# A decoder layer's down projection, from plain matrix products to one level of Strassen in a hand-ordered item list

## The chip, the cores and the metric

One core of a Trainium2 chip runs the whole kernel. The metric is device microseconds of one execution; the time before is the median of three runs. A core has five engines that run side by side and meet at semaphores: TensorE (PE; its weight loads are PEld), VectorE (DVE), ScalarE (ACT), GpSimd (POOL) and SyncE (SP), which here only issues DMAs. TensorE writes its sums to PSUM, 8 banks of 128 x 512 float32; everything else works from SBUF.

## The reference, cut to what matters

One layer: a token mixer (not touched), then a gated feed-forward part on 512 tokens of width 2048, inner width 5632 (44 blocks of 128).

```python
for l in range(DEPTH):                       # DEPTH = 1
    ...
    x = x + rms_norm(m, attn_post_norm[l])
    u = rms_norm(x, ffn_pre_norm[l])
    f = (jax.nn.silu(u @ w_gate[l]) * (u @ w_up[l])) @ w_down[l]
    x = x + rms_norm(f, ffn_post_norm[l])
```

The down projection is the product with w_down, 512 x 5632 by 5632 x 2048. The final norm needs the sum of squares over all 2048 columns of a token before it can scale.

## The kernel before

All inputs are float32, and a product is made of three matmuls: each operand is split into a high part (ScalarE's rounding copy, `wh` for weights) and a remainder (VectorE's subtraction of that copy from the source, `wl`), and high x high, high x remainder and remainder x high are summed in PSUM (`mm3`, lines 120 to 122). `whi` (L100) and `wlo` (L107) do this for a weight tile of 128 x 1024, `split` (L128, L129) for an activation tile of 128 x 512.

*Gate and up* (`bridge`) already use one level of Strassen in Winograd's form: blocks of the two operands are added and subtracted, and seven half-size products take the place of eight. Their order is written by hand: `items` is a list of products, each with a weight source and a function that issues its matmuls, and tables `pre_`, `tops` and `post` hang other work on item numbers. The loop at lines 1159 to 1183 walks the list: at step i it makes the high part of item i + 2, runs `pre_[i]`, runs `tops` up to item i + 3 (weight differences on VectorE), makes the remainder of item i + 2, and then issues item i's matmuls. TensorE, VectorE, ScalarE and GpSimd keep this order; SP's order of DMAs is set by the scheduler. The activated products go out to `hd` in HBM, one 128 x 512 tile for each of the 44 blocks of the inner width (inner width by tokens).

*The down projection* (`down`) follows in ordinary scheduled code. For each of two column halves p of 1024 it walks the 44 blocks k: a weight tile is loaded and split, `hd`'s tile is loaded once and split in each half, and 4 token tiles (tt) x 2 column tiles (c) x 3 matmuls of 128 x 512 add to eight PSUM banks (lines 1230 to 1235). The last six blocks of the second half (`NLAST`) run token tile by token tile, so that the banks of one token tile are done while others still run. `evac` takes a bank's squares (ScalarE, L1215) and its product with the gain (VectorE, L1216); then a token tile's reciprocal root mean square is worked out by small VectorE operations (`rstd`), and four `scalar_tensor_tensor` (L1256) scale and add the residual before the stores (L1258).

Of the kernel before, what the change touches and what calls it, by code (L numbers as in the profile page):

```python
# [25 lines left out]
NEXT = 22  # L26
NR = 3
NHU = 30
# [3 lines left out]
NLAST = 6  # L32
# [30 lines left out]
class Net:  # L63
# [141 lines left out]
    def run(self, ctx):  # L205
# [20 lines left out]
        with tc.tile_pool(name="ext", bufs=NEXT, reuse_waits="tile") as self.M:  # L226
            self.down()
# [625 lines left out]
    def bridge(self, q01, ea):  # L853
# [293 lines left out]
        for u in (*range(NPRE, NUNIT), *range(NPRE)):  # L1147
# [8 lines left out]
            at(pre_, i + 2, hout, u)  # L1156
        srcs, his, los = [], [], []
# [27 lines left out]
    def down(self):  # L1185
        nc, t = self.nc, self.t
        hs = []

        def load(k):
            h = self.u() if k < NHU else self.mx()  # L1190
            nc.sync.dma_start(h, t["hd"][k])
            hs.append(h)

        for k in range(4):
            load(k)
        gr, x2 = [], {}
# [12 lines left out]
        def evac(p, tt, ps):
            if p == 0:  # L1210
                ssc[tt] = self.C.tile([P, 4], F32, name=f"ssc{tt}")
            for c in range(2):
                cc = p * 2 + c
                f = self.u()
                nc.scalar.activation(f, ps[c], AF.Square, accum_out=ssc[tt][:, cc:cc + 1])  # L1215
                nc.vector.tensor_tensor(f, ps[c], gr[cc], op=ALU.mult)  # L1216
                fg[tt, cc] = f

        for p in range(2):
            ps = {tt: (self.acc(), self.aux()) for tt in range(NTT)}  # L1220
            nlast = NLAST if p else 0
            for k in range(FT - nlast):
                wh, wl = self.wsplit(t["wd"][p, k])
                if p == 0 and k + 4 < FT:
                    load(k + 4)
                with self.hp():
                    hh, hl = self.split(hs[k], alloc=self.mx if p or k > 16 else self.u)
                if p == 0 and k == 24:
                    loads()
                for tt in range(NTT):  # L1230
                    ts = slice(tt * P, (tt + 1) * P)
                    for c in range(2):
                        cs = slice(c * 512, (c + 1) * 512)
                        self.mm3(ps[tt][c], hh[:, ts], hl[:, ts], wh[:, cs], wl[:, cs],
                                 k == 0, k == FT - 1)
            if not p:
                for tt in range(NTT):
                    evac(p, tt, ps[tt])
                continue
            last = []  # L1240
            for k in range(FT - nlast, FT):
                with self.hp():
                    st = self.wload(t["wd"][p, k])
                    last.append((self.split(hs[k], alloc=self.mx), [self.split(st[:, :512]),
                                                     self.split(st[:, 512:])]))
# [102 lines left out]
```

## Time and profile before

| | |
|---|---|
| median of 3 runs (lowest, highest) | 2247.0 us (2246.62, 2247.09) |
| span of the profiled execution | 2249.2 us |
| TensorE busy (matmuls), share of the span | 2213.9 us, 98% |
| VectorE busy | 1457.8 us, 65% |
| ScalarE busy | 911.3 us, 41% |
| GpSimd busy | 254.0 us, 11% |
| DMA | 299.86 MB, mean 133 GB/s |
| chain that ended last | PE 90%, DVE 5% |

The profile gives no time of its own for the profiled execution other than its span, which is 2.2 us above the median. Busy time of TensorE counts a matmul from its start to its modelled end, and matmuls overlap, so the spacing of starts tells the price of one, not the duration beside it. The same holds to a lesser degree for VectorE, whose operations start a little before the one ahead has ended.

### The profile page before, as it was taken

The numbers are of one execution on the slowest core, as the hardware profiler recorded it, in microseconds if no ns is written. First come the engines' busy times: TensorE is split into PE (matmuls) and PEld (weight loads), VectorE is DVE, ScalarE is ACT, GpSimd is POOL, SyncE is SP. The second block draws the span as 40 slices with busy tenths as digits, with TensorE's granted clock in tenths as the row PEclk, the third lists the DMA queues.
The fourth block names the chain that finished last, engine by engine and source line by source line (L and its number), as shares of the span: only waits on it lengthen the run. The fifth ranks groups of instructions, "written<-read, shape, count | busy, mean of one in ns | idle before, by whom it ended". The sixth has DMA issues, their size and how long they took to land.

```text
span 2249.2 us, 35218 instructions
## 1 busy us (share of the span) xinstructions
PE 2213.9 (98%) x14150; PEld 2005.5 (89%) x14150; DVE 1457.8 (65%) x2238; ACT 911.3 (41%) x1274; POOL 254.0 (11%) x218
## 2 busy tenths in 40 slices
PE   9999999999999999999999999999999999999998
PEld 7878887888879999999999999999999888888886
DVE  6347777535554577897888778999999623343345
ACT  5324343336553444654444444444343422232231
POOL 2012311000001665530000000000000000000000
PEclk9999899999999999999999999999999999999999
DMA  6222112232103576884333343666655744433332
GB/s 206 93 85 66 57 57 62 94 95 83 66 29 103 183 221 196 251 259 129 118 118 114 119 125 122 186 203 207 188 181 171 253 141 123 130 94 95 102 103 104
DMA packets 108340, 299.86 MB, mean 133 GB/s; under 512 B 12160, under 2 KB 29328, under 8 KB 108176
## 3 DMA queue, kind: packets, MB, share of 16 engines
q1 hardware_dynamic: 105152, 292.10, 41.6%
q10 hardware_dynamic: 3024, 5.51, 0.7%
q8 instruction: 111, 1.82, 0.3%
q14 instruction: 53, 0.43, 0.1%
HBM read 271.34 MB, written 26.21 MB: 132 GB/s over the span
## 4 chain that ended last, share of the span: by engine, by line
PE 90%; DVE 5%; POOL 1%; ACT 1%; issue 1%; DMA 1%; SPq 0%; DVEq 0%; ACTq 0%; POOLq 0%
PE acc L120 18%; PE acc L122 18%; PE acc L121 18%; PE aux L122 10%; PE aux L120 10%; PE aux L121 10%; DVE wl L107 1%; PE aux L541 1%; PE aux L755 1%; DVE u L526 1%; ACT wh L100 0%; DVE u L955 0%; PE aux L588 0%; PE aux L723 0%; PE aux L741 0%
## 5 line engine op out<-in xcount | busy, mean ns | idle before, releaser
L120 PE MATMUL acc<-u,wh 128*128 128x256 f32 (+2 forms) x2064 | 635.0, 309 | 2.6 <-ACT wh L270 1.4
L121 PE MATMUL acc<-u,wh 128*128 128x256 f32 (+2 forms) x2064 | 635.7, 308 | 0.0
L122 PE MATMUL acc<-u,wl 128*128 128x256 f32 (+2 forms) x2064 | 634.6, 308 | 0.1
L107 DVE TENSOR_TENSOR wl<-ws,wh 128x1024 fp32r<-128x1024 f32 (+2 forms) x315 | 375.5, 1193 | 305.2 <-ACT wh L100 299.0
L100 ACT ACTIVATE wh<-ws 128x1024 fp32r<-128x1024 f32 (+1 forms) x315 | 329.9, 1049 | 498.9 <-PE acc L121 141.2
L120 PEld LDWEIGHTS acc<-u,wh 128*128 128x128 f32 (+1 forms) x2064 | 395.5, 192 | 21.4 <-ACT wh L270 1.9
L122 PEld LDWEIGHTS acc<-u,wl 128*128 128x128 f32 (+1 forms) x2064 | 395.4, 192 | 19.1 <-DVE wl L107 1.0
L121 PEld LDWEIGHTS acc<-u,wh 128*128 128x128 f32 (+1 forms) x2064 | 395.8, 192 | 17.9 <-DVE u L250 0.4
L122 PE MATMUL aux<-u,wl 128*128 128x256 f32 (+1 forms) x1264 | 362.3, 287 | 1.9 <-DVE wl L107 1.9
L120 PE MATMUL aux<-u,wh 128*128 128x256 f32 (+1 forms) x1264 | 362.8, 287 | 0.3 <-ACT wh L100 0.3
L121 PE MATMUL aux<-u,wh 128*128 128x256 f32 (+1 forms) x1264 | 362.1, 286 | 0.0
L100 ACT ACTIVATE wh<-wt 128x1024 fp32r<-128x1024 f32 x176 | 186.9, 1062 | 299.1 <-PE aux L121 112.8
L122 PEld LDWEIGHTS aux<-u,wl 128*128 128x128 f32 x1264 | 243.5, 193 | 3.8 <-DVE wl L107 2.5
L120 PEld LDWEIGHTS aux<-u,wh 128*128 128x128 f32 x1264 | 243.6, 193 | 1.8 <-ACT wh L100 0.5
L121 PEld LDWEIGHTS aux<-u,wh 128*128 128x128 f32 x1264 | 243.6, 193 | 1.2
L107 DVE TENSOR_TENSOR wl<-wt,wh 128x1024 fp32r<-128x1024 f32 x176 | 215.0, 1222 | 34.0 <-ACT wh L100 33.9
L120 PE MATMUL acc<-wh,u 128*128 128x512 f32 x356 | 140.2, 395 | 0.0
L121 PE MATMUL acc<-wl,u 128*128 128x512 f32 x356 | 140.1, 394 | 0.0
L122 PE MATMUL acc<-wh,u 128*128 128x512 f32 x356 | 139.5, 394 | 0.0
L120 PE MATMUL acc<-wh,m 128*128 128x512 f32 x260 | 101.1, 389 | 0.0
L121 PE MATMUL acc<-wl,m 128*128 128x512 f32 x260 | 101.1, 389 | 0.0
L122 PE MATMUL acc<-wh,m 128*128 128x512 f32 x260 | 101.1, 389 | 0.0
(293 smaller groups left out, 3037.2 us busy)
## 6 DMA issues: line engine op xcount, KB each, us to landing
ws<-wgu_in SPq DMA_DIRECT2D x136, 512.0 KB, 3.8
wsx<-wgu_in SPq DMA_DIRECT2D x88, 512.0 KB, 3.7
ws<-wd_in SPq DMA_DIRECT2D x88, 512.0 KB, 3.7
ws<-wo_in SPq DMA_DIRECT2D x56, 512.0 KB, 3.7
ws<-wf_in SPq DMA_DIRECT2D x39, 512.0 KB, 3.6
ws<-wt_in SPq DMA_DIRECT2D x32, 512.0 KB, 3.6
hd<-g SPq DMA_DIRECT2D x44, 256.0 KB, 2.8
u<-hd SPq DMA_DIRECT2D x30, 256.0 KB, 3.9
```

The lines of the kernel that those rows point to most:

```text
L100: self.nc.scalar.activation(h, st, AF.Copy)
L107: nc.vector.tensor_tensor(lo[:, :d], st[:, :d], h[:, :d], op=ALU.subtract)
L120: mm(ps, lhsT=ah, rhs=bh, start=start, stop=False)
L121: mm(ps, lhsT=ah, rhs=bl, start=False, stop=False)
L122: mm(ps, lhsT=al, rhs=bh, start=False, stop=stop)
L526: nc.vector.tensor_tensor(qt[hs].rearrange("p (c h n s) -> p c h n s", c=NTT, h=2, s=s)[:, :, h], c3(v3(q)[:, :, 1, :]), c3(dv[:, :, 1, :] ...
L541: mm(ps[:m, c * 64:(c + 1) * 64], lhsT=kt[:, c * P:c * P + m], rhs=qt[:, c * 64:(c + 1) * 64], start=True, stop=True)
L755: mm(po[:, ts], lhsT=v[kt][:, (h % 4) * P:(h % 4 + 1) * P], rhs=pT[:, kt * P:(kt + 1) * P], start=kt == 0, stop=kt == tt)
```

## The change

The down projection becomes part of the item list. `down` and its pool are gone; `down_items` appends to `items` after the last unit of gate and up. Four blocks of the inner width make a "duo": its first and third block are one half of the inner width, its second and fourth the other, so that activations (tokens in halves of 256) and weights (columns in halves of 512, in each column half p of 1024) are 2 x 2 blocks. Eleven duos are taken two at a time in six chunks (the last has one), and for each chunk and each p come seven products in the order 1, 5, 6, 3, 7, 4, 2, each for all its duos. A product of one duo is one item: 12 matmuls of 128 x 512 into two banks. Two pairs of banks, X and Z, hold running sums, and a third pair per p collects product 2 over all chunks. At the end of a product its sum is taken from PSUM and added to one of 16 accumulators in SBUF (`evac`): by ScalarE's copy to a buffer of `gv` (four of them) and GpSimd's addition, for product 7 by VectorE straight from PSUM. The activation sums S1 to S4 (`ssum...`) and one weight difference in four (product 7) are GpSimd's; three are VectorE's. `conv` splits the activations once per duo, not once per p. At the end `stat` takes the squares and multiplies by the gain (GpSimd, for the last block VectorE), and `final` scales and stores a token tile.

```diff
-        with tc.tile_pool(name="ext", bufs=NEXT, reuse_waits="tile") as self.M:
-            self.down()
...
             at(pre_, i + 2, hout, u)
+        self.down_items(items, pre_, post, tops, at)
...
-    def down(self):
+    def down_items(self, items, pre_, post, tops, at):
...
+        def ssum13(d):
+            r = raw[d]
+            r["S1"] = self.u()
+            G.tensor_tensor(r["S1"], r["21"], r["22"], op=ALU.add)
+            G.tensor_tensor(r["21"], r["11"], r["21"], op=ALU.subtract)
+            r["S3"] = r.pop("21")
...
+        def tsum(c, p, d, n):
+            w = lambda q: W[c, p, d, q]
+            if n == 5:
+                o = w("11") if len(chunks[c]) > 1 else wtile("wt")
+                D.tensor_tensor(o, w("12"), w("11"), op=ALU.subtract)
...
+            elif n == 7:
+                G.tensor_tensor(w("12"), w("22"), w("12"), op=ALU.subtract)
...
+        def prod(c, p, n, d):
+            def f(wh, wl):
...
+                ps = bank["X" if n in (1, 6, 7) else p if n == 2 else "Z"]
...
+                for tt in range(2):
+                    for j in range(2):
+                        a = slice(j * 256 + tt * P, j * 256 + (tt + 1) * P)
+                        w = slice(j * 512, (j + 1) * 512)
...
+                        mm(hi, wh, first and j == 0, False)
+                        mm(hi, wl, False, False)
+                        mm(lo, wh, False, last and j == 1)
+            return f
+
+        EV = {1: ("C11",), 5: ("C22",), 6: ("C12",), 3: ("C12",), 7: ("C22", "C21"), 4: ("C21",)}
+
+        def evac(c, p, n):
+            ps = bank["X" if n in (1, 6, 7) else "Z"]
+            for name in EV[n]:
+                for tt in range(2):
+                    a = acc.get((p, name, tt))
+                    if a is None:
+                        a = acc[p, name, tt] = self.u()
+                        nc.scalar.copy(a, ps[tt])
+                    elif n != 7:
+                        g = self.gv()
+                        nc.scalar.copy(g, ps[tt])
+                        G.tensor_tensor(a, a, g, op=ALU.add)
+                    else:
+                        D.tensor_tensor(a, ps[tt], a, op=ALU.add)
...
+            if name == "C11":
+                D.tensor_tensor(f, bank[p][tt], f, op=ALU.add)
+            sq = self.gv()
+            nc.scalar.activation(sq, f, AF.Square, accum_out=ssc[tok][:, cc:cc + 1])
+            (eng or G).tensor_tensor(f, f, gr[cc], op=ALU.mult)
...
+        end = len(items)
+        at(pre_, end - 15, tail_loads)
...
+        for tok in (2, 3):
+            at(pre_, end, final, tok)
+        for tt in range(2):
+            at(pre_, end + 1, stat, 1, "C11", tt, D)
+        for tok in (0, 1):
+            at(pre_, end + 1, final, tok)
```

VectorE in the middle of the down projection, before: `wl` is a weight remainder, `m` the remainder of an activation tile.

```order
L107 TENSOR_TENSOR wl_19348<-ws_19344,wh_19346 128x1024
L107 TENSOR_TENSOR wl_19384<-ws_19380,wh_19382 128x1024
L129 TENSOR_TENSOR m_19681<-u_19494,m_19680 128x512
L107 TENSOR_TENSOR wl_19420<-ws_19416,wh_19418 128x1024
L129 TENSOR_TENSOR m_19717<-u_19570,m_19716 128x512
```

And of the change, in a chunk with two duos: L126 is `split`'s remainder, L104 the weight remainder, L1255 the difference t4, L1296 the addition of product 7's sum from PSUM (`acc`).

```order
L126 TENSOR_TENSOR u_20804<-u_20689,u_20803 128x512
L1255 TENSOR_TENSOR wt_20505<-wt_20662,wt_20505 128x1024
L104 TENSOR_TENSOR wl_20808<-wsx_20556,wh_20801 128x1024
L1255 TENSOR_TENSOR wt_20528<-wt_20681,wt_20528 128x1024
L104 TENSOR_TENSOR wl_20836<-wt_20505,wh_20822 128x1024
L126 TENSOR_TENSOR u_20853<-u_20714,u_20852 128x512
L104 TENSOR_TENSOR wl_20860<-wt_20528,wh_20850 128x1024
L1296 TENSOR_TENSOR u_18787<-acc_18680,u_18787 128x512
L1296 TENSOR_TENSOR u_18789<-acc_18681,u_18789 128x512
```

Beside the remainders, three weight differences in four and two accumulators' additions of every chunk and p now stand in VectorE's queue.

GpSimd's queue before ends in the output projection, ahead of gate and up: these are its last rows.

```order
L109 TENSOR_TENSOR wl_9449<-ws_9432,wh_9434 128x256
L109 TENSOR_TENSOR wl_9498<-ws_9477,wh_9479 128x256
L109 TENSOR_TENSOR wl_9536<-ws_9526,wh_9528 128x256
L109 TENSOR_TENSOR wl_9576<-ws_9564,wh_9566 128x256
L1344 UNCONDITIONAL_BRANCH
L1344 ISA
```

With the change 188 operations follow there; these are from one half of a chunk (L1294 an accumulator's addition, L1252 the weight difference of product 7, L1204 and L1205 the sums S1 and S3).

```order
L1294 TENSOR_TENSOR u_18729<-u_18729,g_20683 128x512
L1294 TENSOR_TENSOR u_18731<-u_18731,g_20686 128x512
L1252 TENSOR_TENSOR wsx_20530<-ws_20558,wsx_20530 128x1024
L1294 TENSOR_TENSOR u_18787<-u_18787,g_20739 128x512
L1294 TENSOR_TENSOR u_18789<-u_18789,g_20742 128x512
L1252 TENSOR_TENSOR wsx_20556<-ws_20580,wsx_20556 128x1024
L1294 TENSOR_TENSOR u_18832<-u_18832,g_20778 128x512
L1294 TENSOR_TENSOR u_18834<-u_18834,g_20781 128x512
L1204 TENSOR_TENSOR u_20784<-u_20691,u_20693 128x512
L1205 TENSOR_TENSOR u_20691<-u_20689,u_20691 128x512
```

GpSimd had nothing behind the output projection; now it has work through the whole down projection, all of it reading two tiles of SBUF.

VectorE at the end, before: the last token tile's bank products and the start of its norm (ahead of them the last scaling of the token tile before; `rstd`'s small operations and four scalings follow).

```order
L1256 SCALAR_TENSOR_TENSOR u_21829<-u_21829,sm_21838,u_19530 128x512
L1216 TENSOR_TENSOR u_21895<-acc_20274,u_19504 128x512
L1216 TENSOR_TENSOR u_21898<-aux_20275,u_19506 128x512
L1253 TENSOR_REDUCE sm_21901<-ssc_20261 128x1
L168 TENSOR_SCALAR sm_21903<-sm_21901 128x1
```

And of the change: L1326 scales the last tiles of token tile 3, L1314 adds product 2's bank to C11, L1317 is the gain.

```order
L1326 SCALAR_TENSOR_TENSOR u_18789<-u_18789,sm_22312,u_21895 128x512
L1326 SCALAR_TENSOR_TENSOR u_19109<-u_19109,sm_22312,u_21897 128x512
L1314 TENSOR_TENSOR u_19069<-aux_19316,u_19069 128x512
L1317 TENSOR_TENSOR u_19069<-u_19069,u_21877 128x512
L1314 TENSOR_TENSOR u_19071<-aux_19317,u_19071 128x512
L1317 TENSOR_TENSOR u_19071<-u_19071,u_21877 128x512
L1321 TENSOR_REDUCE sm_22341<-ssc_22116 128x1
```

Before, one token tile is left behind the last matmul; now token tiles 2 and 3 stand in VectorE's queue ahead of C11, and token tiles 0 and 1 behind it.

## Rows read from the trace of the kernel before

**Rows 1.** Busy us by stage: length, PE, PEld, DVE, ACT, POOL, clock, DMA share, GB/s
```profile
1400.00:1700.00 300.00, 300.00 (x2502) 300.00 (x2502) 275.58 (x340) 123.90 (x130) 0.00 (x0) 1.00 0.62 192
1762.00:2200.00 438.00, 438.00 (x1934) 362.75 (x1934) 157.55 (x172) 133.38 (x179) 0.00 (x0) 1.00 0.42 128
2200.00:2249.20 49.20, 39.59 (x175) 32.48 (x173) 26.28 (x84) 6.53 (x18) 0.00 (x0) 0.94 0.23 86
```

**Rows 2.** Timeline of PE: start, us, engine, line, operation, out<-in
```profile
1758.03 0.40 PE L120 MATMUL acc<-wh,u 128*128 128x512 f32 x1
...
1759.19 0.28 PE L122 MATMUL aux<-u,wl 128*128 128x256 f32 x1
...
1761.82 0.40 PE L120 MATMUL aux<-wh,u 128*128 128x512 f32 x1
...
2239.21 0.39 PE L122 MATMUL aux<-u,m 128*128 128x512 f32 x1
```

**Rows 3.** Groups by line, 1762 to 2239: count | busy us, mean ns | idle before
```profile
L107 DVE TENSOR_TENSOR wl<-ws,wh 128x1024 fp32r<-128x1024 f32 x80 | 98.0, 1226 | 105.9 <-ACT wh L100 105.8
L1216 DVE TENSOR_TENSOR u<-acc,u 128x512 f32<-128x512 f32 x7 | 4.8, 686 | 16.6 <-ACT u L1215 16.6
L100 ACT ACTIVATE wh<-ws 128x1024 fp32r<-128x1024 f32 x80 | 84.2, 1052 | 131.1 <-PE aux L122 124.1 <-DMA ws<-wd_in 4.4 <-PE aux L121 2.5
L129 DVE TENSOR_TENSOR m<-u,m 128x512 fp32r<-128x512 f32 x43 | 29.3, 691 | 105.6 <-ACT m L128 102.6 <-PE aux L121 3.0
```

**Rows 4.** Timeline of DVE where POOL does nothing
```profile
854.53 0.47 DVE L989 SCALAR_TENSOR_TENSOR u<-u,col,r 128x256 f32<-128x256 f32 x1
...
861.32 0.95 DVE L107 TENSOR_TENSOR wl<-ws,wh 128x768 fp32r<-128x768 f32 x1
...
1738.21 1.22 DVE L1024 TENSOR_TENSOR wt<-wsx,wt 128x1024 f32<-128x1024 f32 x1
1739.35 1.22 DVE L107 TENSOR_TENSOR wl<-wt,wh 128x1024 fp32r<-128x1024 f32 x1
...
1752.35 1.29 DVE L129 TENSOR_TENSOR u<-u,u 128x512 fp32r<-128x512 f32 x2
```

**Rows 5.** Timeline of POOL where DVE does nothing
```profile
745.00 1.29 POOL L884 TENSOR_TENSOR m<-m,u 128x512 f32<-128x512 f32 x1
```

**Rows 6.** Timeline of DVE, then of POOL, where they meet
```profile
735.29 1.48 DVE L107 TENSOR_TENSOR wl<-ws,wh 128x1024 fp32r<-128x1024 f32 x1 [2.80 <-ACT wh L100]
736.69 0.74 DVE L911 TENSOR_TENSOR u<-aux,u 128x256 f32<-128x256 f32 x2
...
738.01 2.34 DVE L107 TENSOR_TENSOR wl<-ws,wh 128x1024 fp32r<-128x1024 f32 x1
...
735.63 2.27 POOL L884 TENSOR_TENSOR m<-m,u 128x512 f32<-128x512 f32 x1
737.99 1.29 POOL L885 TENSOR_TENSOR u<-u,m 128x512 f32<-128x512 f32 x1
```

**Rows 7.** Timeline of DVE, then of POOL, both without a gap
```profile
898.84 1.48 DVE L107 TENSOR_TENSOR wl<-ws,wh 128x768 fp32r<-128x768 f32 x1
900.24 1.84 DVE L955 SCALAR_TENSOR_TENSOR u<-u,col,rm 128x256 f32<-128x256 f32 x2
902.00 1.49 DVE L107 TENSOR_TENSOR wl<-ws,wh 128x768 fp32r<-128x768 f32 x1
...
898.59 2.32 POOL L957 TENSOR_TENSOR u<-hq,u 128x256 f32<-128x256 f32 x2
900.87 0.93 POOL L109 TENSOR_TENSOR wl<-ws,wh 128x256 fp32r<-128x256 f32 x1
```

**Rows 8.** Timeline of the end: last token tile's reduction and scalings
```profile
2240.96 0.15 DVE L1253 TENSOR_REDUCE sm<-ssc 128x1 f32<-128x4 f32 x1
...
2243.46 2.74 DVE L1256 SCALAR_TENSOR_TENSOR u<-u,sm,u 128x512 f32<-128x512 f32 x4
```

**Rows 9.** Busy us by stage, columns as in rows 1
```profile
830.00:840.00 10.00, 6.93 (x59) 6.72 (x57) 2.63 (x8) 4.48 (x9) 3.21 (x3) 1.00 0.75 248
840.00:850.00 10.00, 8.14 (x47) 8.17 (x48) 5.26 (x17) 3.11 (x6) 4.83 (x5) 0.66 0.41 136
```

More of the change, by code (lines that the diff above doesn't have):

```diff
@@ L25 @@
 NMIX = 15
-NEXT = 22
 NR = 3
-NHU = 30
 NEA = 8
@@ L31 @@
 NUNIT = FT
-NLAST = 6
 LOGEXP = "natural_log_exp_and_others"
@@ new lines, in down_items, with sload @@
+        base = len(items)
+        duos = [NPRE + 4 * d for d in range((FT - NPRE) // 4)] + [4 * d for d in range(NPRE // 4)]
+        chunks = [duos[i:i + 2] for i in range(0, len(duos), 2)]
+        nchunk = len(chunks)
+        S, raw, W = {}, {}, {}
+        acc = {}
+        bank = {}
+        gr, x2, ssc = {}, {}, {}
+        D, G = nc.vector, nc.gpsimd
+        def sload(d):
+            r = raw[d] = {}
+            for n, e, hs in (("11", 0, 0), ("21", 0, 256), ("22", 1, 256), ("12", 1, 0)):
+                r[n] = self.u()
+                nc.sync.dma_start(
+                    r[n].rearrange("p (k s) -> p k s", k=2),
+                    t["hd"][d + e:d + 4:2].rearrange("k p s -> p k s")[:, :, hs:hs + 256])
@@ new lines, in final @@
+        def final(tok):
+            ss = self.sm(1)
+            D.reduce_sum(ss, ssc[tok], axis=mybir.AxisListType.X)
+            r = self.rstd(ss, D_, 1)
+            row, tt = tok // 2, tok % 2
+            for cc in range(4):
+                f = acc[cc % 2, f"C{row + 1}{cc // 2 + 1}", tt]
+                D.scalar_tensor_tensor(f, f, r, x2[tok, cc], op0=ALU.mult, op1=ALU.add)
+                nc.sync.dma_start(self.out[tok * P:(tok + 1) * P, cc * 512:(cc + 1) * 512], f)
+        D_ = 2048
@@ new lines, in down_items @@
+        end = len(items)
+        at(pre_, end - 15, tail_loads)
+        done = {0: ("C12", "C22", "C21", "C11")}
+        for k, name in enumerate(done[0]):
+            for tt in range(2):
+                at(pre_, end - 6 + k, stat, 0, name, tt)
+        for name, o in (("C12", -2), ("C22", -1), ("C21", 0)):
+            for tt in range(2):
+                at(pre_, end + o, stat, 1, name, tt)
+        for tok in (2, 3):
+            at(pre_, end, final, tok)
+        for tt in range(2):
+            at(pre_, end + 1, stat, 1, "C11", tt, D)
@@ L1309, in _layout @@
                                     ).reshape(FT, 4, P, 1024)
+    order = [NPRE + 4 * d for d in range((FT - NPRE) // 4)] + [4 * d for d in range(NPRE // 4)]
     a["wd"] = np.ascontiguousarray(
-        f["w_down"][0].reshape(FT, P, 2, 1024).transpose(2, 0, 1, 3))
+        f["w_down"][0].reshape(FT // 4, 2, 2, P, 2, 2, 512)[[k // 4 for k in order]]
+        .transpose(5, 0, 2, 4, 3, 1, 6)).reshape(2, FT // 4, 4, P, 1024)
     a["w2"] = np.ascontiguousarray(f["gla_gate_w2"][0])
```

167 lines of the change are left out of this document (102 added, 65 removed).

## Prediction
> **What bounds the kernel now.** I read the busy time by stage first [rows 1]. In gate and up and in the down projection TensorE is busy for the whole stretch at a granted clock of 1.00, that is 2.4 GHz. In the down projection VectorE works 157.6 of 438.0 us, ScalarE 133.4, GpSimd nothing. So TensorE is the bound of this stage, and the engines that feed it have more than half of their time free. The only part without TensorE is the end: 9.6 us from the last matmul's end to the end of the span.
>
> TensorE's price per matmul comes from the timeline [rows 2]. The down projection's first matmul starts at 1758.03; five of them run ahead of the last 2.63 us of gate and up (1759.19 to 1761.82). As if sorted, down starts at 1758.03 + 2.63 = 1760.7 and ends at 2239.21 + 0.39 = 2239.6: 478.9 us for 2 x 44 x 4 x 2 x 3 = 2112 matmuls of 128x512, 0.2268 us each, without a hole.
>
> Then I read what the free engines charge alone [rows 3 to 5] and against each other [rows 6, 7], because the change gives GpSimd work beside a busy VectorE, which the down projection of before never does.
>
> **The change, part by part.** *TensorE, removed.* Eleven groups of four k blocks ("duos"), 2 column halves, 7 products, 12 matmuls each: 1848. That is 264 fewer, 264 x 0.2268 = 59.9 us. A product (one item) takes 12 x 0.2268 = 2.72 us; a chunk of two duos has 28 items, 76.2 us. Six matmuls in a row into one bank instead of three cost nothing: gate and up sends 24 in a row and makes 2502 in 300 us, 0.12 each [rows 1].
>
> *VectorE, added.* In a full chunk 28 weight remainders (L104) and 12 weight differences at 1024 columns, 1.14 us from start to start (1738.21, 1739.35) [rows 4], 45.6 us; 14 activation remainders at 512 columns, two in 1.29 where one takes 0.69 [rows 3, 4], so 0.60 from start to start, 8.4 us. Together 54.0. Eight additions from PSUM at 0.69 [rows 3] come on top; an operation that reads PSUM keeps its time under a GpSimd operation (two at 736.69 take 0.74 beside GpSimd's 735.63 to 737.90) [rows 6], so they hide there and count nothing. If VectorE were alone, 59.5 of 76.2 would hide under TensorE.
>
> *ScalarE, added.* 28 conversions at 1.05 [rows 3], and 14 conversions and 20 copies of half the width, at most the same: 65 of 76.2 us. Hidden.
>
> *GpSimd, added.* In a full chunk 20 accumulator additions and 8 activation sums at 128x512, and 4 weight differences at 128x1024. Alone a 128x512 takes 1.29 [rows 5]; for 1024 there is no row, I take 2.4, a little under twice. That is 46 of 76.2 us, and alone would hide too.
>
> *Their meeting decides.* A remainder of 1024 columns takes 1.23 us alone [rows 3], but 2.34 when GpSimd's 128x512 has started just before it (737.99 against 738.01) [rows 6]: 1.11 longer. The other way round, GpSimd's 1.29 becomes 2.27 when VectorE came first [rows 6]: 0.98 longer, about what VectorE still had to do. So they take turns. The long case has both engines full [rows 7]: every 3.16 us (898.84 to 902.00) VectorE does one remainder of 768 and two products of 256, and GpSimd three operations of 256. Alone VectorE's three take 0.95 + 2 x 0.47 = 1.89 [rows 4]; the other 1.27 went to GpSimd, 0.42 an operation, 0.85 for 512 columns. VectorE's starts lie closer than its times by some 0.08 (1.14 against 1.22) [rows 4]; with that it is 0.50, or 1.0 for 512. So a GpSimd 128x512 costs VectorE 0.85 to 1.11 us; I take 1.0, and twice that for 1024.
>
> A full chunk then costs VectorE 54.0 + 28 x 1.0 + 4 x 2.0 = 90.0 us, against 76.2 of TensorE: **VectorE becomes the bound**. Chunk 0 has 8 accumulator additions (first sums are copies) and 22 activation remainders: 45.6 + 13.2 + 24 = 82.8. Chunk 4 prepares one duo only: 45.6 + 4.2 + 32 = 81.8. Chunks 0 to 4: 82.8 + 3 x 90.0 + 81.8 = 434.6, less about 6 since two items are prepared ahead: 428.6, where TensorE alone needs 5 x 76.2 = 381. With 0.85 or 1.11 for the 164 units of 512 it is 404 or 447.
>
> *The last chunk and the end.* The last chunk is one duo, 14 items, 38.1 us of TensorE. In it GpSimd has 30 operations up to the last sum of C21 (28 of 512, 2 of 1024): 28 x 1.30 + 2 x 2.4 = 41.2, after about 4 us for the first item and its copy, and 20 VectorE operations of 1024 columns stand in their way at 0.98: 19.6. Sum 64.8. Products wait for these additions, since four buffers carry the copies from PSUM to GpSimd. Behind the 30th: four more on GpSimd, 5.2; three scalings of token tile 2 at 0.69, 2.1; token tile 3 whole, 5.2 (from reduction to the last of four scalings, 2240.96 to 2246.20) [rows 8]; C11's addition, square (about 0.6, a little over half of 1.05) and gain for two tiles, 4.0; token tiles 0 and 1, 10.4; the last store, 2246.20 to 2249.2, 3.0. Sum 29.9. The whole is 94.7, where 38.1 + 9.6 = 47.7 would stand with the end of before. Without any meeting it is 75.1.
>
> *Ahead of the stage.* In the last 13 items of gate and up, where VectorE is at 92% (275.6 of 300) [rows 1], 8 sums on GpSimd come in, and activation remainders fall from some 9 to 6. That is 8 x 1.0 less 1.8; with two items of lead I take 2 us (0 to 6).
>
> *SP.* The 20 tail loads stand ahead of the last three weight loads in its queue. Their buffers come free some items before the last chunk, and the queue's rate here is 128 GB/s where gate and up moved 192 [rows 1]. I take zero, up to 3 us.
>
> **Sum.** 1760.7 + 2 + 428.6 + 94.7 = 2286.0. It is made against the profiled span, 2249.2, which is 2.2 above the median of the runs, 2247.0; on the runs' scale 2284. The bounds of the terms give some 2238 to 2312.
>
> **Rivals.** *TensorE stays the bound: faster.* The mechanism would be that GpSimd does the waiting and VectorE's work stays near its own 54.0 per chunk. It decides where a GpSimd 128x512 costs VectorE under (76.2 - 54.0) / 36 = 0.62 us. Then 1760.7 + 381 + 75.1 = 2217, 2215 on the runs' scale. For it: 17 us of VectorE per chunk are free, and GpSimd does lose time too (0.98). Against it: the stretch with both engines full shows 0.85 at the least. Chance 0.13.
>
> *GpSimd holds the other out for its whole length: slower still.* Then 1.29 counts in place of 1.0, 164 x 0.29 = 47.6 more, 2332. Against it stand 1.11 and 0.85, both less than the length. Chance 0.05.
> The Trainium skill, "SBUF — State Buffer", section "Who interferes with whom", says that a VectorE instruction with two SBUF inputs contends with a GpSimd instruction that reads SBUF, and that whoever issues first has the shared ports for the whole instruction. The trace agrees that they shut each other out and that a PSUM operand spares VectorE, but 1.11 and 0.85 are less than the whole 1.29; by that sentence taken literally the time would be the 2332 above.
>
> *ScalarE waits for GpSimd's sums.* S4 is summed one item ahead of its conversion (L1215 against L126), in GpSimd's queue behind two additions and a weight difference: 3 x 2.1 + 3.1, some 9 us, against 6.5 of two items. That is 3 us twice per chunk, most of it time in which GpSimd has its turn anyway: up to 20 us, 2304. TensorE's clock belongs here: after 6.93 busy us of 10 the granted clock fell to 0.66 for the next 10 [rows 9]. The full chunks would be 85% busy, the last one 60%; but at 0.66 an item takes 4.1 us, still under the 4.6 that GpSimd sets there. Chance 0.07.
>
> **How the numbers follow.** The forecast has 0.75, the rivals 0.13, 0.05 and 0.07. The range 2228 to 2322 leaves out the first rival but for its upper edge, the second, and the forecast's far ends, some 0.18. Faster by over 0.2% (under 2242.5) takes the first rival and a little of the forecast's lower end, 0.14; within 0.2%, about what a measurement here can tell from no change, 0.03; slower 0.83.
>
> **What would show it.** Right: VectorE near 95% busy from the stage's start into the last chunk, its 1024-column remainders at 1.8 us on average, GpSimd's 512-column additions near 2, TensorE with gaps that end on the remainder (L104), a full chunk in 87 to 93 us, and 25 us or more between the last matmul and the end. Wrong: remainders near 1.25, 76 us a chunk and TensorE without gaps; that would be the first rival. Long waits of ScalarE for S4 would be the third. If GpSimd's 1024-column difference is far from 2.4, the terms shift by 22 times the error.

## The result and the profile after

The changed kernel takes 2351.1 us (2349.0 to 2351.7), the kernel before 2246.8 on the same chip: ratio 1.0461, 95% interval 1.0446 to 1.0476. The forecast was 2284 with a range up to 2322: the sign is right, and the time lies 67 us above it.

Busy time by stage of the changed kernel, columns as in [rows 1]: chunk 0, the three full chunks, chunk 4, the last chunk up to its last matmul, and the end.

```profile
1759.10:1855.50 96.40, 82.53 (x338) 64.53 (x337) 82.81 (x66) 53.12 (x75) 42.30 (x20) 0.96 0.36 113
1855.50:1957.50 102.00, 84.62 (x337) 65.64 (x336) 89.73 (x63) 46.63 (x62) 64.73 (x32) 0.93 0.33 105
1957.50:2059.90 102.40, 84.87 (x338) 65.62 (x337) 90.11 (x63) 46.62 (x62) 64.74 (x32) 0.93 0.33 103
2059.90:2162.20 102.30, 84.73 (x338) 65.61 (x336) 90.01 (x63) 46.62 (x62) 64.75 (x32) 0.93 0.34 103
2162.20:2255.80 93.60, 82.31 (x337) 65.58 (x336) 80.82 (x57) 41.85 (x54) 56.45 (x28) 0.93 0.32 99
2255.80:2309.60 53.80, 43.22 (x169) 32.83 (x167) 43.75 (x30) 28.27 (x49) 49.52 (x26) 0.94 0.22 80
2309.60:2349.70 40.10, 0.00 (x0) 0.00 (x0) 26.02 (x76) 5.89 (x18) 12.78 (x11) 0.55 0.28 105
```

Where [rows 1] show TensorE busy for the whole stage, no engine is busy throughout a chunk now. Read the third number behind the length, VectorE: 82.8, 89.7, 90.1, 90.0 and 80.8 us of work. The prediction had 82.8, 90.0 three times, and 81.8. VectorE's work came out within 1 us in every chunk, but each chunk is 12 to 14 us longer than that work. Chunks 0 to 4 take 496.7 us against 428.6 in the sum (68.1 more), the last chunk and the end 93.9 against 94.7.

The whole difference to the kernel before, made up from TensorE's dense 76.2 us per chunk and 47.7 for the last chunk with the old end: chunk 0 costs 20.2 more, the full chunks 25.8, 26.2 and 26.1, chunk 4 17.4, the last one with the end 46.2; the stage starts 1.6 earlier and TensorE has 59.9 less to do. That is 161.9 - 1.6 - 59.9 = 100.4, and the spans differ by 2349.7 - 2249.2 = 100.5.

Groups by line of the changed kernel in the three full chunks (count | busy us, mean ns | idle before), which answer to [rows 3 to 5]:

```profile
L1294 POOL TENSOR_TENSOR u<-u,g 128x512 f32<-128x512 f32 x60 | 106.5, 1796 | 112.2 <-ACT g L1293 112.2
L104 DVE TENSOR_TENSOR wl<-wt,wh 128x1024 fp32r<-128x1024 f32 x61 | 104.2, 1720 | 0.0
L126 DVE TENSOR_TENSOR u<-u,u 128x512 fp32r<-128x512 f32 x42 | 47.2, 1123 | 36.1 <-ACT u L125 36.1
L1252 POOL TENSOR_TENSOR wsx<-ws,wsx 128x1024 f32<-128x1024 f32 x12 | 38.9, 3246 | 0.0
L104 DVE TENSOR_TENSOR wl<-ws,wh 128x1024 fp32r<-128x1024 f32 x12 | 34.1, 2858 | 0.0
L1296 DVE TENSOR_TENSOR u<-acc,u 128x512 f32<-128x512 f32 x24 | 14.8, 678 | 0.0
```

The remainder L104 takes 1.72 and 2.86 us where alone it takes 1.23 [rows 3], GpSimd's addition 1.80 where alone it takes 1.29 [rows 5], and its 1024-column difference t3 (L1252) 3.25. VectorE's additions from PSUM (L1296) keep 0.68. So both are held up, as the prediction had it. What it did not have is the idle time in L126's row: 36.1 us in three chunks, 12.0 of the 12.3 that VectorE idles per chunk, all of it waiting for ScalarE's half of an activation split (L125). Waits of the same stretch (us in total, times, longest):

```profile
PE acc L1273 <- DVE wl L104: 49.2, 26, 5.7
DVE u L126 <- ACT u L125: 36.1, 24, 3.9
ACT wh L97 <- DVE wt L1255: 34.3, 12, 3.7
ACT wh L97 <- DVE wt L1245: 31.0, 12, 3.4
ACT u L125 <- POOL u L1215: 28.1, 6, 5.8
ACT wh L97 <- POOL wsx L1252: 13.9, 3, 4.7
```

ScalarE, in turn, waits for GpSimd: 28.1 us for S4 (L1215), 13.9 us for t3. It waits longer in total for VectorE's own weight differences, which it has to convert. So which of VectorE's waits stand behind GpSimd has to be read from the timeline. It shows such a place behind S4; first GpSimd, then ScalarE, then VectorE:

```profile
2018.20 2.27 POOL L1294 TENSOR_TENSOR u<-u,g 128x512 f32<-128x512 f32 x1
2020.43 3.38 POOL L1252 TENSOR_TENSOR wsx<-ws,wsx 128x1024 f32<-128x1024 f32 x1
2023.78 3.96 POOL L1294 TENSOR_TENSOR u<-u,g 128x512 f32<-128x512 f32 x2
2027.70 2.83 POOL L1252 TENSOR_TENSOR wsx<-ws,wsx 128x1024 f32<-128x1024 f32 x1
2030.49 2.27 POOL L1215 TENSOR_TENSOR u<-u,u 128x512 f32<-128x512 f32 x1
2032.72 2.97 POOL L1294 TENSOR_TENSOR u<-u,g 128x512 f32<-128x512 f32 x2
2035.65 2.26 POOL L1215 TENSOR_TENSOR u<-u,u 128x512 f32<-128x512 f32 x1
...
2032.79 0.63 ACT L125 ACTIVATE u<-u 128x512 fp32r<-128x512 f32 x1 [5.79 <-POOL u L1215]
2037.95 0.63 ACT L125 ACTIVATE u<-u 128x512 fp32r<-128x512 f32 x1 [3.58 <-POOL u L1215]
...
2028.22 3.39 DVE L104 TENSOR_TENSOR wl<-ws,wh 128x1024 fp32r<-128x1024 f32 x1
2033.45 1.11 DVE L126 TENSOR_TENSOR u<-u,u 128x512 fp32r<-128x512 f32 x1 [1.84 <-ACT u L125]
2038.61 0.69 DVE L126 TENSOR_TENSOR u<-u,u 128x512 fp32r<-128x512 f32 x1 [1.84 <-ACT u L125]
```

GpSimd works without a gap from 2018.2 to 2037.9, and S4 stands in that queue; ScalarE stands still 5.79 and 3.58 us, and VectorE idles behind it, 1.84 us each time. The same chunk has one place behind t3:

```profile
1978.15 3.37 POOL L1252 TENSOR_TENSOR wsx<-ws,wsx 128x1024 f32<-128x1024 f32 x1
1981.55 1.06 ACT L97 ACTIVATE wh<-wsx 128x1024 fp32r<-128x1024 f32 x1 [4.62 <-POOL wsx L1252]
1983.16 1.39 DVE L126 TENSOR_TENSOR u<-u,u 128x512 fp32r<-128x512 f32 x1 [3.90 <-ACT u L125]
```

So 3.90 + 2 x 1.84 = 7.6 of the chunk's 12.1 us stand behind GpSimd. In the others ScalarE had waited for VectorE's difference or for TensorE, or had its two copies (L1293) ahead of the conversion.

### The profile page after: what moved, and what is told of

Its sections match the earlier page's. It is cut to its first block, busy times and chain, and to the rows that moved or that the text cites. A ratio compares the mean times of both kernels' runs of the same rounds, so it can differ in the third digit from the quotient of the medians.

```text
span 2349.7 us, 35375 instructions
## 1 busy us (share of the span) xinstructions
PE 2194.8 (93%) x13886; PEld 1967.2 (84%) x13886; DVE 1778.2 (76%) x2387; ACT 1032.9 (44%) x1447; POOL 628.7 (27%) x406
## 4 chain that ended last, share of the span: by engine, by line
PE 69%; DVE 14%; POOL 6%; issue 5%; ACT 3%; DMA 2%; SPq 0%; DVEq 0%; ACTq 0%; POOLq 0%
PE acc L117 14%; PE acc L118 14%; PE acc L119 14%; PE aux L119 6%; PE aux L117 6%; PE aux L118 6%; DVE wl L104 6%; PE acc L1273 4%; POOL u L1294 2%; DVE wt L1255 1%; POOL wsx L1252 1%; DVE u L126 1%; ACT wh L97 1%; ACT u L125 1%; DMA ws<-wo_in 1%
## 5 line engine op out<-in xcount | busy, mean ns | idle before, releaser
L97 ACT ACTIVATE wh<-wt 128x1024 fp32r<-128x1024 f32 x286 | 303.1, 1061 | 494.3 <-PE aux L118 110.9
L104 DVE TENSOR_TENSOR wl<-ws,wh 128x1024 fp32r<-128x1024 f32 (+2 forms) x255 | 331.3, 1301 | 197.6 <-ACT wh L97 197.1
L97 ACT ACTIVATE wh<-ws 128x1024 fp32r<-128x1024 f32 (+1 forms) x255 | 267.2, 1049 | 391.9 <-PE acc L118 158.4
L104 DVE TENSOR_TENSOR wl<-wt,wh 128x1024 fp32r<-128x1024 f32 x286 | 399.1, 1400 | 39.7 <-ACT wh L97 39.4
L1273 PE MATMUL acc<-wh,u 128*128 128x512 f32 x1056 | 346.8, 409 | 5.9 <-ACT g L1293 5.9
L1273 PE MATMUL acc<-wl,u 128*128 128x512 f32 x528 | 222.8, 422 | 76.8 <-DVE wl L104 76.8
L1273 PEld LDWEIGHTS acc<-wh,u 128*128 128x128 f32 x1056 | 210.3, 199 | 51.6 <-ACT g L1293 7.2
L1294 POOL TENSOR_TENSOR u<-u,g 128x512 f32<-128x512 f32 x108 | 192.6, 1806 | 187.0 <-ACT g L1293 187.0
L1273 PEld LDWEIGHTS acc<-wl,u 128*128 128x128 f32 x528 | 105.5, 200 | 120.7 <-DVE wl L104 99.5
L126 DVE TENSOR_TENSOR u<-u,u 128x512 fp32r<-128x512 f32 x85 | 86.1, 1018 | 63.4 <-ACT u L125 63.4
```

What stands on the lines that cost most here:

```text
L97: self.nc.scalar.activation(h, st, AF.Copy)
L104: nc.vector.tensor_tensor(lo[:, :d], st[:, :d], h[:, :d], op=ALU.subtract)
L126: self.nc.vector.tensor_tensor(lo, src, hi, op=ALU.subtract)
L1273: mm = lambda l, r, st, sp: nc.tensor.matmul(ps[tt], lhsT=l[:, a], rhs=r[:, w], start=st, stop=sp, skip_group_check=True)
L1294: G.tensor_tensor(a, a, g, op=ALU.add)
```

## Experiments

Two theories were set against each other. **Theory 1:** the additions and differences on GpSimd take VectorE's time, and that alone is the cost. **Theory 2:** the cost is lateness: GpSimd's results come too late for engines that issue in order with two items of lead. Times below are medians; all were measured beside runs of the kernel before, whose median was 2246.8 to 2248.1 each time. Of the forecasts in the texts below, theory 1's came true in e1, e3 and e4; neither theory's did in e2, e5, e6 and e10. e11 came out at the price of the prediction, e12 at its second forecast, and e14 and e15 0.7 and 4.6 us above the nearest of theirs.

**e1_s4_early**: the sum S4 two items earlier.

```diff
-                            at(pre_, b0 + 5 + k, ssum4, d)
+                            at(pre_, b0 + 3 + k, ssum4, d)
...
-                                    at(pre_, b0 + 2 * o + k, conv, d, KIND[n])
+                                    at(pre_, b0 + (2 if n == 6 else 2 * o) + k, conv, d, KIND[n])
```

> Only the place of one step is changed: GpSimd sums S4 of the next chunk's duos two items earlier, so that ScalarE's conversion of S4, which in the trace of the changed kernel waited up to 5.8 us for that sum, finds it done (S2's conversion, which must precede the sum, moves up with it). Theory 1 (GpSimd's instructions take VectorE's time, and that alone makes the chunk long): no difference, 2351 within 4 us, since the same instructions run. Theory 2 (VectorE has work enough for the chunk, but idles some 12 us per full chunk, because ScalarE stands in order behind the S4 sum and the rings lead by two items only): 6 waits of 28.1 us in all over three chunks, so some 9 us per chunk; five chunks give up to 45 us, at least 10, thus 2305 to 2340.

Measured 2354.0. ScalarE's wait for S4 is gone from the list of waits in its full chunks, but the others moved up; waits in the three full chunks of that kernel:

```profile
PE acc L1273 <- DVE wl L104: 46.5, 23, 5.7
DVE u L126 <- ACT u L125: 32.4, 20, 3.9
ACT wh L97 <- POOL wsx L1252: 15.8, 5, 4.7
ACT wh L97 <- DVE wl L104: 7.4, 2, 5.6
```

VectorE waits 32.4 us in place of 36.1, and the time is the same. So ScalarE's longest single wait was worth nothing by itself: other waits came in its place.

**e5_t3_early**: t3 two items earlier as well. In the last chunk, which has one duo, t3 now overwrites its input before t1 has read it, so values there change; the instructions are the same.

```diff
-                            at(tops, i - 2, tsum, c, p, d, n)
+                            at(tops, i - 4, tsum, c, p, d, n)
```

> The run with the earlier S4 sum gave 2354, no gain: in its trace ScalarE's waits on S4 were gone, but waits on GpSimd's weight difference t3, which stands behind the sum and the additions in GpSimd's order, took their place (up to 5.7 us). Here t3 is also made two items earlier, ahead of the first additions, where GpSimd stood idle 6.5 us; the same instructions run. Theory 2, as it now stands (GpSimd's own stretch of sums, differences and additions, each drawn out to 2.2 to 3.4 us beside VectorE, is the chain that ScalarE and TensorE wait for in a third of each half): the stretch starts some 6 us earlier, so up to 6 us per half or 12 per chunk come back, four chunks and the short ones: 2300 to 2340. Theory 1 alone (only the sum of VectorE's time counts): 2351 within 4 us.

Measured 2359.1: not the gain of theory 2. Busy time of the two halves of the first full chunk of that kernel, columns as in [rows 1]:

```profile
1859.00:1906.80 47.80, 40.45 (x169) 30.85 (x168) 47.35 (x31) 21.63 (x28) 36.76 (x17) 1.00 0.40 129
1906.80:1961.30 54.50, 44.32 (x170) 34.34 (x168) 46.05 (x33) 24.65 (x34) 30.01 (x16) 0.91 0.27 83
```

In the first half VectorE is now busy 47.35 of 47.8 us: the idle time there was filled, by instructions that GpSimd held up for longer (93.4 us of work in the chunk, 89.7 before). Moving GpSimd's work in time, by two items, returns nothing.

**e2_no_adds**: GpSimd's 108 additions left out.

```diff
                         nc.scalar.copy(g, ps[tt])
-                        G.tensor_tensor(a, a, g, op=ALU.add)
```

> Left out: the 108 additions by which GpSimd adds a copied product to an SBUF accumulator (the ScalarE copies stay, the sums are missing from the output). Theory 1: 20 additions per full chunk at 1.0 us of VectorE's time each leave VectorE with 90 - 20 = 70 us per chunk, under TensorE's 76; the chunk falls from 102 to 76 to 82 us, five chunks give back 100 to 130 us, the time is 2220 to 2250. Theory 2 alone (the waits on S4 and the short lead): the S4 sums and the duo sums stay where they are, GpSimd only has less ahead of them, so at most the 12 us of idle time per chunk come back, about 60 us: 2290 or more. Rival 3 (the additions cost nothing, and the time lies in the ScalarE copies or the changed order of the loads): 2351 within 5.

**e11_adds_twice**: each addition followed by a second one into scratch.

```diff
                         G.tensor_tensor(a, a, g, op=ALU.add)
+                        G.tensor_tensor(g, a, g, op=ALU.add)
```

> Each of GpSimd's 108 additions is followed by a second one of the same size into its own scratch tile, which nobody waits for but the next user of that tile. Sum of both engines' times (theory 1 as it now stands): 108 x 1.29 = 139 us more, 2490, between 2475 and 2505. The price of the prediction, 1.0 us each: 2459, between 2448 and 2472. The price that leaving the additions out showed, 0.76 us each: 2433, between 2420 and 2445. Theory 2 alone (only the chain of late inputs costs): less than 40 us more, since no step of that chain waits for the second additions except by GpSimd's order.

Measured 2268.6 without and 2467.8 with twice the additions. A full chunk of each:

```profile
1934.30:2021.60 87.30, 80.13 (x338) 63.50 (x337) 75.36 (x63) 46.53 (x62) 30.67 (x12) 0.98 0.38 121
```

```profile
1987.10:2109.90 122.80, 91.11 (x338) 69.36 (x336) 92.95 (x63) 46.57 (x62) 96.67 (x53) 0.86 0.28 85
```

The additions cost (2351.1 - 2268.6) / 108 = 0.76 us each, and a second set (2467.8 - 2351.1) / 108 = 1.08 each, near the prediction's 1.0 and away from the full 1.29. Of the 20 us that the second set adds to a chunk, VectorE's work takes only 3; the rest is idle time, now 30 us per chunk. Leaving the additions out does the opposite: of the 15.1 us by which the chunk becomes shorter, 14.7 are VectorE's work, 0.74 per addition, and its idle time stays at 11.9 of 87.3 us. This idle time is not GpSimd's: by the starts and ends in the trace GpSimd is at work in only 0.9 us of it. Most of it is again VectorE waiting for ScalarE, which still makes the copies; in the chunk shown:

```profile
DVE u L126 <- ACT u L125: 9.4, 8, 2.0
```

**e10_one_input**: in place of the additions GpSimd multiplies the copy by 1.0 into the accumulator, an instruction with one SBUF input.

```diff
-                        G.tensor_tensor(a, a, g, op=ALU.add)
+                        G.tensor_scalar(a, g, 1.0, None, op0=ALU.mult)
```

> In the changed kernel GpSimd's 108 additions of two SBUF operands become 108 multiplications of one SBUF operand by 1.0 (the copied product overwrites the accumulator: the sums are left out of the output). GpSimd keeps as many instructions, places and waits. Theory 1 as the runs so far have it (a GpSimd instruction of two SBUF inputs and a VectorE one exclude each other, so that a chunk takes the sum of both engines' times: VectorE's own 56.6 us + 28 x 1.29 + 4 x 2.45 = 102.5, measured 102.2): one input takes nothing from VectorE, and the time is that of the run without the additions, 2262 to 2285. Theory 3 (whatever GpSimd does takes VectorE's time, or the additions' places and waits in GpSimd's order are what costs): 2330 to 2352.

Measured 2300.3, between the two. A full chunk, and GpSimd's group in three of them:

```profile
1943.90:2033.80 89.90, 79.69 (x337) 63.51 (x336) 74.11 (x63) 46.52 (x62) 61.84 (x32) 0.98 0.38 120
```

```profile
L1294 POOL TENSOR_SCALAR u<-g 128x512 f32<-128x512 f32 x60 | 118.3, 1986 | 85.3 <-ACT g L1293 85.3
```

VectorE's work is 74.1 us in all, no more than without any additions (75.4). But the multiplication is not free for it. The first two lines show a meeting of the two engines, the third two multiplications while VectorE does nothing:

```profile
2000.33 1.94 POOL L1294 TENSOR_SCALAR u<-g 128x512 f32<-128x512 f32 x1
2000.85 1.63 DVE L104 TENSOR_TENSOR wl<-ws,wh 128x1024 fp32r<-128x1024 f32 x1
2256.53 2.94 POOL L1294 TENSOR_SCALAR u<-g 128x512 f32<-128x512 f32 x2
```

A remainder takes 1.63 us here where alone it takes 1.23 [rows 3]: 0.4 longer, where a two-input operation of the same size made it 1.11 longer [rows 6]. The multiplication takes 1.47 alone and 1.99 on average, and what stands behind it in GpSimd's queue is late: VectorE idles 15.8 us in this chunk. So 51 of the 83 us go with the second input and 32 stay with the multiplications. About half of the 32 lies ahead of the last chunk; its 48.5 us and an end of 41.6, against 41.2 and 33.4 without additions, make up 15.5. How the 32 divide between VectorE held up and inputs that come late is not shown.

**e3_adds_dve**: the additions on VectorE, straight from PSUM. **e12_adds_dve_sbuf**: on VectorE, from ScalarE's copy in SBUF.

```diff
-                    elif n != 7:
-                        g = self.gv()
-                        nc.scalar.copy(g, ps[tt])
-                        G.tensor_tensor(a, a, g, op=ALU.add)
                     else:
                         D.tensor_tensor(a, ps[tt], a, op=ALU.add)
```

```diff
                         nc.scalar.copy(g, ps[tt])
-                        G.tensor_tensor(a, a, g, op=ALU.add)
+                        D.tensor_tensor(a, a, g, op=ALU.add)
```

> All of the work is done, but the 108 additions are VectorE's, straight from PSUM into the accumulator in place of a ScalarE copy and a GpSimd addition. Theory 1: an addition with its input in PSUM took VectorE 0.62 to 0.75 us also beside a busy GpSimd, against the 1.0 us that it loses to a GpSimd addition; VectorE's work per chunk is 90 - 20 x 1.0 + 20 x 0.65 = 83 us, the chunk 83 to 93, the time 2255 to 2305: moving work back to the engine that is the bound makes the kernel faster. Theory 2: VectorE has the additions in its own in-order queue and the stalls on S4 stay: no better than 2335, perhaps slower. Rival 3 (VectorE cannot take more): 20 x 0.65 = 13 us per chunk more on the bound, 2351 + 70 = 2420.

> ScalarE still copies each product out of PSUM, and VectorE, not GpSimd, adds the copy to the accumulator from SBUF; the run with VectorE adding straight from PSUM gave 2283. Sum of both engines' times: a 128x512 addition takes VectorE 0.69 us from either place, so 56.6 + 20 x 0.69 + 8 x 1.29 + 4 x 2.45 = 90.5 per chunk as there, 2280 to 2292. If it was the PSUM operand that made the additions cheap (it can run beside GpSimd), these meet GpSimd's remaining sums and differences: 20 x 0.4 us per chunk more at most, 2300 to 2330.

Measured 2283.2 from PSUM and 2310.5 from SBUF. The additions' group in three full chunks, first from PSUM, then from SBUF:

```profile
L1292 DVE TENSOR_TENSOR u<-acc,u 128x512 f32<-128x512 f32 x84 | 53.2, 680 | 0.0
```

```profile
L1294 DVE TENSOR_TENSOR u<-u,g 128x512 f32<-128x512 f32 x60 | 48.5, 849 | 11.5 <-ACT g L1293 11.5
```

Handing 108 additions back to the busiest engine makes the kernel 68 us faster. From SBUF an addition takes 0.85 in place of 0.68 us, and VectorE waits 11.5 us for the copies. So the PSUM operand itself, and the ScalarE step that it saves, are worth 27 of the 68 us.

**e4_all_dve**: as e3, with `D, G = nc.vector, nc.vector`: GpSimd does nothing in the down projection.

> As the run with the additions on VectorE, and the rest of GpSimd's work in the down projection (sums of the hidden units' half blocks, the weight difference t3, the products with the gain) is VectorE's too: GpSimd is idle there. Theory 1: per full chunk 8 sums of 128x512 cost VectorE 0.6 to 0.7 us in place of 1.0, 4 differences of 128x1024 1.2 in place of 2.0; VectorE has 77 us, level with TensorE's 76; the chunk is 77 to 85 us and the time 2225 to 2270, better than the run before it by 15 to 35 us. Theory 2: in-order VectorE has yet more in its one queue, the stalls stay: 2330 or more. Rival 3: 2420 or more.

Measured 2249.6, ratio to the kernel before 1.0009 (1.0000 to 1.0018). A full chunk, and chunk 4:

```profile
1929.30:2011.30 82.00, 78.11 (x338) 62.56 (x337) 80.65 (x95) 36.91 (x42) 0.00 (x0) 1.00 0.40 128
2093.20:2169.40 76.20, 76.20 (x337) 62.96 (x336) 75.73 (x85) 33.40 (x35) 0.00 (x0) 1.00 0.38 125
```

Now VectorE is the bound in the full sense: 80.65 of 82.0 us. And chunk 4 is the clearest row of the study: VectorE has 75.73 us of work in 76.2 us, and TensorE runs dense. Two items of lead are enough there, with nothing from GpSimd and without ScalarE's copies.

**e6_t3_dve**: the changed kernel with only the 22 differences t3 on VectorE. **e14_t3_too**: e3 with t3 on VectorE. **e15_sums_too**: e3 with the 44 sums S1 to S4 on VectorE (in the same way, in `ssum13`, `ssum2`, `ssum4`).

```diff
-                G.tensor_tensor(w("12"), w("22"), w("12"), op=ALU.subtract)
+                D.tensor_tensor(w("12"), w("22"), w("12"), op=ALU.subtract)
```

> Only the 22 weight differences t3 (128x1024) go from GpSimd to VectorE, in the same place of the order; the additions and the half-block sums stay GpSimd's. Theory 1 by price alone: VectorE does one in 1.22 us and by the prediction loses 2.0 us to GpSimd's, so 22 x 0.8 = 17 us less: 2334. Theory 2 (GpSimd's stretch is the chain): 3.3 us of GpSimd's are taken out of that stretch twice per half and nothing waits for t3 there, 5 to 9 us per half: 2265 to 2315.

> All of the work is done. As the run with VectorE adding straight from PSUM (2283), and the 22 weight differences t3 are VectorE's too; GpSimd keeps only the half-block sums and the products with the gain. By price alone (2.0 us lost to a GpSimd difference against 1.22 for an own one): 17 us less, 2266. If VectorE's 5 us of idle time per chunk stand behind t3 (the wait of weight conversion on GpSimd): they go too, 20 to 30 us, and the chunk comes to 83: 2250 to 2258, all of the step to the run with GpSimd idle. If they stand behind the sums: 2266 to 2272.

> All of the work is done. As the run with VectorE adding straight from PSUM (2283), and the 44 half-block sums S1 to S4 are VectorE's too; GpSimd keeps only the 22 differences t3 and the products with the gain. By price alone (1.0 us lost to a GpSimd sum against 0.69): 44 x 0.3 = 13 us less, 2270. If VectorE's 5 us of idle time per chunk stand behind the sums (splits waiting for S1 to S4): 2250 to 2260. If they stand behind t3: 2268 to 2275.

Measured 2326.9 (24.3 less than the changed kernel), 2258.7 (24.5 less than e3) and 2279.6 (3.6 less than e3). A full chunk of e3, of e6, of e14 and of e15:

```profile
1938.20:2029.50 91.30, 80.80 (x338) 63.40 (x337) 85.18 (x83) 36.54 (x42) 29.70 (x12) 0.98 0.37 116
```

```profile
1948.50:2045.30 96.80, 81.86 (x337) 62.84 (x336) 90.56 (x67) 46.51 (x62) 52.95 (x28) 0.98 0.34 108
```

```profile
1931.80:2015.60 83.80, 79.01 (x338) 62.39 (x338) 81.39 (x87) 36.67 (x42) 17.26 (x8) 1.00 0.40 127
```

```profile
1938.90:2027.70 88.80, 80.50 (x338) 63.56 (x337) 85.26 (x91) 36.65 (x42) 13.01 (x4) 0.98 0.37 119
```

Each t3 on GpSimd costs the kernel 1.1 us more than on VectorE, with the additions beside it or without. In e6 VectorE's work even rises a little (90.6), since it does 12 more differences in three chunks, and its idle time falls from 12.3 to 6.2 us: e6's gain is idle time. From e3 to e14 the work falls by 3.8 and the idle time from 6.1 to 2.4 (the other two full chunks of e3 have 4.6 and 4.8). Moving the sums gains little, 0.08 us each, though there are twice as many.

**e7_best** and **e13_best2**: versions built on e4, meant to beat both kernels. The single duo is the first chunk, the last half ends on other products, two token tiles share one inverse root; e13 also prepares the second chunk earlier.

```diff
-        chunks = [duos[i:i + 2] for i in range(0, len(duos), 2)]
+        chunks = [duos[:1]] + [duos[i:i + 2] for i in range(1, len(duos), 2)]
...
+        LAST = (1, 5, 6, 3, 2, 7, 4)
...
-            r = self.rstd(ss, D_, 1)
+            r = self.rstd(ss, D_, 2)
```

> The run with all of GpSimd's work on VectorE (2249.6 us), and then: the single duo is the first chunk and not the last; in the last half the products come in the order 1, 5, 6, 3, 2, 7, 4, so that the first two token tiles can be finished under TensorE's last items; the inverse root is taken for two token tiles at once. By that run's trace: first chunk two halves of 21 us, four full chunks at 82, the last at 76 to 82, and a tail of 14 to 20 us in place of 30. 1761 + 42 + 4 x 82 + 78 + 18 = 2227, between 2222 and 2242. If VectorE is the bound to the end (it has 468 us of work of the 489 in the projection and its tail, and none is taken away but two chains of the inverse root, 5 us): not under 1761 + 463 = 2224.

> As the run with the single duo first (2245.6), where the second half of the first chunk and the first half of the next took 25.2 and 47.0 us against 21 and 40.6, because the preparation of the second chunk's half-block sums was crowded there; now that preparation begins up to 12 items earlier, under gate and up. VectorE the bound: 8 to 10 us less, 2236 to 2240. If gate and up have no room for it on VectorE, the gain is given back ahead of the stage: 2244 to 2247.

Measured 2245.6 and 2246.4, ratios 0.9994 (0.9985 to 1.0003) and 0.9998 (0.9989 to 1.0007): no difference from the kernel before, and some 18 and 8 us above what was expected of them. In e7 the end shrank from 30.0 to 22.5 us, but the first chunk (48.2 in place of 42) and the second (88.4 in place of 82) gave it back, because VectorE had the preparation of two duos there. In e13 the first half of the first chunk became 3.0 us longer, the next two halves 2.8 and 3.7 shorter, and the stage began 2.3 later. In e7 VectorE works 464.0 of the 486.8 us from the stage's start to the end, so a better order alone could win 22.8 us at most.

## Why the prediction was wrong

**Right.** TensorE's saving and item time: chunk 4 of e4 runs at 76.2 us. The last chunk and the end: 93.9 against 94.7, with GpSimd busy 49.5 of the 53.8 us up to the last matmul, as argued; at the prediction's own border, the end of the last addition into C21 (2317.5), it is 61.7 + 32.2 in place of 64.8 + 29.9. Long waits of ScalarE for S4, the sign of the third rival, did show.

**Right in number.** VectorE's work: 433.5 us over chunks 0 to 4 against 434.6 in the sum, by two sizes that cancelled (below). The price of a GpSimd addition: the second set costs 1.08 us each against 1.0, but that is the kernel's time. VectorE's work, which the prediction meant, rises by 0.14 per second addition (e11) and by 0.74 per first one (e2). Ahead of the stage no 2 us were lost: down starts at 1759.1.

**The step that failed: "VectorE becomes the bound", 90.0 us of work taken for 90.0 us of time.** The sum of VectorE's work is a length only if VectorE never waits. It waits 12 to 14 us in every chunk, 63.2 us over chunks 0 to 4; with the 6 us of lead that did not show up as a shorter stage, and 1.1 us less work, that is 63.2 + 6 - 1.1 = 68.1, the miss of that stretch. "VectorE near 95% busy" was the prediction's own sign of being right, and 88% of a full chunk is what the rows show.

**Why it waits.** Shown: in a full chunk 7.6 of the 12.0 us that VectorE waits for ScalarE stand behind t3 and S4 on GpSimd (the two timelines above). The idle time per chunk falls from 12.3 us to 6.2 without t3 on GpSimd, to 6.1 with the additions straight from PSUM, to 2.4 with both, to 1.4 with nothing on GpSimd (e6, e3, e14, e4). Shown too: it is not the place of a single step (e1, e5), and not the lead of two items as such (chunk 4 of e4). Not all of it is GpSimd's. e3, e14 and e4 also lose ScalarE's copies; with the copies and without additions (e2) it is 11.9 us, with the copies and VectorE's additions (e12) 7.9. In chunk 0 some 9.5 of the 13.6 us remain in e4. What ScalarE's copies alone are worth, with the additions left on GpSimd, was not tried. TensorE's lower clock (0.93) is hardly the cause: TensorE itself waits 49.2 us in the three chunks for remainders.

**A rival that the runs leave standing: the two engines take turns.** By the starts and ends in the trace, VectorE or GpSimd is at work for all but 2.7 us of a full chunk, and GpSimd for 9.6 of the 12.3 us that VectorE idles. If a GpSimd unit of 512 columns takes 1.11 us from the pair [rows 6], held or idle, then 36 of them and VectorE's own 59.3 us (estimated below) make 59.3 + 40.0 = 99.3, and 2.7 with neither at work give 102.0, where 102.2 is measured. The same sum gives 121.5 for e11's chunk (56 units), 94.9 for e6's (28, and four differences of 1.14 on VectorE) and 77.1 for e2's (16); VectorE or GpSimd is at work for 120.8, 95.0 and 76.2 us there. It is less good for e3 and e14 (89.1 and 84.7 against 85.6 and 81.3). By this account the 12.2 us that a full chunk is longer than 90.0 are 5.3 for PSUM additions that did not hide, 4.0 for the price (36 x 0.11) and 2.7 with neither at work, and lateness is no cost of its own. That moving GpSimd's work gained nothing (e1, e5) fits it. The sum with the full 1.29, which the expectation of e10 has, fits the changed kernel too (102.5) but not e11 (139 us expected, 117 measured).

**The third rival** named a wait of this kind, ScalarE waiting for S4, and sized it at up to 20 us in all, "most of it time in which GpSimd has its turn anyway". ScalarE's wait measured 9.4 us per full chunk, where the prediction had 3 us twice, but only 3.7 us of VectorE's idle time stand behind it, and without it the time was the same (e1).

**Two sizes that cancelled.** VectorE's eight PSUM additions were to hide under GpSimd's work and count nothing; they stand in its busy time at 0.68 each. GpSimd's 36 units were to cost VectorE 1.0 each. From e4's 80.65 us, less what moved there at the start-to-start times of the prediction (28 x 0.60 + 4 x 1.14 = 21.4), VectorE's own work is 59.3 with those additions, an estimate, so the 36 units cost (90.0 - 59.3) / 36 = 0.85 of its work, the lower bound of the prediction.

**The first rival** (TensorE stays the bound) needed a GpSimd instruction to cost under 0.62 us. It does not, by either measure. The second (a hold for the whole length, 1.29) gives 2332 by its own sum, nearer to the result than the forecast, but at too high a price: doubling the additions costs 1.08 each and not 1.29.

**Left open.** It is open whether GpSimd's late results cost time beyond its turns. Without additions (e2) VectorE idles 11.9 us though GpSimd works only 30.7 of 87.3; with the additions on VectorE (e3) and the same GpSimd work it idles 4.6 to 6.1. Why moving the sums gains so much less per instruction than moving t3 (0.08 against 1.1 us) is argued only: VectorE is held up by either, but ScalarE converts t3 within two items, and a remainder that met t3 took 3.39 us (at 2028.22).

**Where the 59.9 us of TensorE go with nothing on GpSimd.** In e4, chunk 0 takes 9.9 more than 76.2, three full chunks 5.8 each, the last chunk with the end 81.0 against 47.7: 9.9 + 17.4 + 33.3 = 60.6. Fewer products, paid back in VectorE work and in a longer end.

## What to carry to other kernels

An engine's summed work is a lower bound of a stage, not its length: before you take it for the length, follow the inputs that it and its suppliers wait for in order, and add what comes late. Work given to GpSimd beside a VectorE that reads two SBUF operands was not free here: a second addition cost 1.08 us of the kernel's time, a little of it as VectorE's work and most as its idle time. Doing it on VectorE, straight from PSUM where the operand is there (0.68 us), can be the cheaper way even when VectorE is the busiest engine. A long wait in the trace is a gain only if the next input is not as late: try it by moving one step before building on it.

## What the hardware showed that was not expected

- GpSimd's multiplication with one SBUF input took 1.47 us where VectorE did nothing, longer than the addition with two (1.29 [rows 5]), and 1.99 on average beside VectorE. It held up VectorE's 1024-column operations less: of 72 that met only such multiplications in e10, 42 kept 1.2 us and 25 took 1.6; of 58 that met only additions in the changed kernel, 16 kept 1.2 and 38 took 2.3.
- GpSimd's 128x1024 difference took 3.25 us beside VectorE, and a remainder of VectorE that met it 3.39 where 1.23 is its time alone; the shorter meetings in the rows of before showed 1.11 us of delay at most.
- With TensorE waiting inside the chunks (84.9 of 102.4 us busy) its granted clock was 0.93 on average, and 0.86 with twice the additions (91.1 of 122.8 us busy), where it was 1.00, that is 2.4 GHz, in e4's chunks (78.1 of 82.0).
